# A hybrid block in split fp32 on one core: row factor one weight unit sooner, plain units made elsewhere

## The chip, the cores and the metric

The kernel runs on one core of one Trainium2 chip. The metric is device microseconds of one execution, as a median over runs. The chip's engines work from queues of their own: TensorE (PE in the profile, with its weight loads as PEld), VectorE (DVE), ScalarE (ACT), GpSimd (POOL), and SyncE (SP), which here issues the weight loads as DMAs.

## The reference

The input is 256 rows of 2048 values, in fp32, as are all weights. One layer is computed, and a last norm:

```python
x = x + 0.5 * swiglu_ffn(rms_norm(x, ffn1_norm), w_gate, w_up, w_down)   # d_ff = 5632
z = rms_norm(x, mix_norm) @ w_in                                         # 2048 x 5120
y = concat(rms_norm(lru part of z), rms_norm(short-convolution part of z))
x = x + y @ w_out
x = x + 0.5 * swiglu_ffn(rms_norm(x, ffn2_norm), ...)
return rms_norm(x, final_norm)

rms_norm(x, gain) = x * rsqrt(mean(x * x) + 1e-6) * gain
swiglu_ffn(x)     = (silu(x @ w_gate) * (x @ w_up)) @ w_down
```

The recurrent part of the mixer needs softplus(-lambda) of a parameter vector of 1024 values.

## The kernel before, in words

**Split fp32.** A product of two fp32 matrices is made from three matmuls of rounded parts: each operand is hi + lo, where ScalarE casts hi and VectorE subtracts to get lo. Weights come in units of four 128-row blocks by 512 columns (1 MB, tile `raw`); `parts_of` makes `hi` (two casts of 128x1024) and `lo` (one subtraction of 128x2048, in FFN1's opening two of 128x1024), and `multiply` issues the matmuls: for each of the two row tiles 4 x 2 with hi and 4 with lo. A unit for both row tiles is 24 matmuls of 128x512. The rows of x (2048 columns = 16 blocks = 4 units) lie transposed in `xT[u]`, each unit as hi and lo side by side.

**The norm.** `Norm.turn` transposes x on PE into PSUM (`pt`); ScalarE writes hi from there, times the gain, VectorE lo. `Norm.squares` sums the squares on ScalarE (`junk`). `Norm.factor` makes the row factor r, one value for each row of x, by a square root on ScalarE (`s`) and small steps on VectorE. `Norm.rows` spreads r over the partitions: two steps on VectorE make diagonals (`diag`), matmuls with ones make `pb`, and VectorE copies it to `bc`.

**An FFN.** The first 512 columns of gate and up are made from xT that is not yet normalised (u = 0..3, each first with gate, then with up: g0, u0, g1, ... in the text); r is applied to the result. The other ten blocks of 512 columns go by pairs, five times `seven` for gate and for up, every second time followed by `down`. `seven` computes 2 row tiles x 2 column blocks over two units of x by seven products instead of eight, as in Strassen's scheme (p0 to p6 in the names), and the other two units as usual (x0, x1 in the names, with the column block behind). For the products it needs the first two units normalised and four sums of them; `seven_of` makes the sums and their hi and lo parts (`xs`). `normalise(u)` makes a unit normalised: per row tile it adds hi and lo into an fp32 tile `v`, multiplies by bc, casts hi and subtracts lo (`x`). On the weights' side, `seven` subtracts raw units from one another on VectorE (`raw <- raw, raw`). Each seven has four PSUM banks a, c, e, d.

**Order.** A tile scheduler reorders instructions within each engine by its own estimates; `Engine.pinned` keeps the written order, in FFN1's opening up to unit 1's up block. Small work for later is put into a queue by `defer` with a cost, and `pump` takes from it after each weight unit; `flush` empties it. In FFN1's opening x itself is being loaded, and transposes and squares of unit u+1 go between weight units; in FFN2's they have been deferred from the mixer's end. `turns` are the transposes of the parameter vectors, called in FFN1 after the second pair, and `prepare` computes the softplus and halves two biases, deferred to the mixer. The buffers: raw units 3 (and 2 kept in an FFN), hi and lo 2 each (and 1 more in an FFN), PSUM 8 banks.

All instructions carry line 42 in the profile, that of the wrapper that records them; they are told apart by tile names, in which the profile leaves out numbers.

Of the kernel before, what the change touches and what calls it, by code (L numbers as in the profile page):

```python
# [48 lines left out]
def hybrid_block(ctx: ExitStack, tc: tile.TileContext, a: dict, out: bass.AP):  # L49
# [157 lines left out]
    class Norm:  # L207
# [12 lines left out]
        def turn(self, ks):  # L220
            for k in ks:
# [8 lines left out]
                act.activation(hi, pt, AF.Copy, scale=g)  # L230
                dve.scalar_tensor_tensor(lo, pt, g, f32(hi), op0=ALU.mult, op1=ALU.subtract)
# [76 lines left out]
    def seven_of(x0, x1, v, spare, parts):  # L308


        a11, a12, a21, a22 = v[0, 0], v[0, 1], v[1, 0], v[1, 1]
        dve.tensor_tensor(spare, a21, a22, op=ALU.add)
        dve.tensor_tensor(a21, a11, a21, op=ALU.subtract)
        dve.tensor_tensor(a11, spare, a11, op=ALU.subtract)
        dve.tensor_tensor(a12, a12, a11, op=ALU.subtract)
        sf = {0: stationary(x0, 0), 1: stationary(x1, 0), 3: stationary(x1, 1)}
        for (i, q), (hi, lo) in zip(((4, spare), (5, a11), (6, a21), (2, a12)), parts):
            act.copy(hi, q)
            dve.tensor_tensor(lo, q, f32(hi), op=ALU.subtract)
            sf[i] = [(hi[:, j, :], lo[:, j, :]) for j in range(UK)]  # L320
        return sf
# [4 lines left out]
    def seven(w, rows, cols, sf, xs, name, keep, done, between=None):  # L326
# [32 lines left out]
        s5 = snap(c, "s5")  # L359
        usual(0, b2, 1, (e, 1, True, not two), (c, 0, False, False))  # L360
        if between:
            between()
        dve.tensor_tensor(w11, w22, w11, op=ALU.subtract)
        product_of(5, w11, a)
        u2 = snap(a, "u2")
        if two:
# [16 lines left out]
    def ffn(tag, norm, after, opening=False):  # L383
        with tc.tile_pool(name=f"ffn{tag}", bufs=1) as fp:
# [32 lines left out]
            xs, vs, sf = [], {}, {}  # L417

            def normalise(u):

                xs.append(big(f"x{tag}_{u}"))
                for t in range(NT):
                    hi, lo = (slice(o + t * P, o + (t + 1) * P) for o in (0, S))
                    v = vs[t, u] = quad(keep(f"v{tag}_{u}_{t}"))
                    x = f32(norm.xT[u])
                    dve.tensor_tensor(v, x[:, :, hi], x[:, :, lo], op=ALU.add)
                    dve.tensor_tensor(v, v, norm.bc[:, hi].unsqueeze(1).to_broadcast([P, UK, P]), op=ALU.mult)
                    act.copy(xs[u][:, :, hi], v)
                    dve.tensor_tensor(xs[u][:, :, lo], v, f32(xs[u][:, :, hi]), op=ALU.subtract)
                if u == 1:  # L430
                    pair = [big(f"xs{tag}_{i}") for i in range(2)]
                    sf.update(
                        seven_of(
                            xs[0], xs[1],
                            vs,
                            quad(keep(f"spare{tag}")),
                            [(b[:, :, o : o + P], b[:, :, o + P : o + S]) for b in pair for o in (0, S)],
                        )
                    )

            ps = {(m, t): bank(f"ps_{m}{tag}_0_{t}") for m in "gu" for t in range(NT)}
            Engine.pinned = opening
            for u in range(KD // UK):
                for m, w in (("g", wg), ("u", wu)):
# [17 lines left out]
                    if opening and u < 3 and m == "u":  # L462
                        norm.turn(range(4 * u + 4, 4 * u + 8))
                        if u == 0:
                            norm.squares(0)
                        norm.squares(u + 1)
                        if u == 2:
                            norm.factor()
                    multiply([(ps[m, t], stationary(norm.xT[u], t), u == 0, u == 3) for t in range(NT)], blk)
                    pump(1.5)  # L470
                    if (u, m) == (1, "u"):
                        Engine.pinned = False
                        flush()
                        if not opening:
                            norm.factor()
                    elif (u, m) == (2, "u" if opening else "g"):
                        norm.rows()
                        normalise(0)
                    if u == 3:
                        for k in range(len(xs), len(xs) + 2):  # L480
                            if k < 4:
# [421 lines left out]
```

## Time and profile before

| | |
|---|---|
| median of 3 runs | 1771.69 us (1770.08 to 1773.82) |
| the profiled execution | 1770.94 us, its span 1769.0 us |
| mean granted clock of TensorE | 0.995 |
| PE, DVE, ACT busy | 98%, 85%, 59% of the span |
| moved by DMA | 343 MB, mean 194 GB/s |

Times in the timelines are in us from the start of the span. An entry in brackets is the time for which the engine sat idle ahead of the instruction, and the engine and tile that released it. FFN1 lies from 0 to 724 us, the mixer to 1049, and FFN2 behind it.

### The profile page before, as it was taken

What the parts mean: (1) busy time and instruction counts of PE and PEld (TensorE: products, weight loads), DVE (VectorE), ACT (ScalarE), POOL (GpSimd) and SP (SyncE); (2) the same over time, 40 slices, a digit from 0 to 9 for tenths busy, and PEclk for the clock granted to TensorE, in tenths of its full rate; (3) what the DMA queues carried; (4) which work ended last, traced back from release to release, by engine and by line L of the source; (5) the groups of instructions that cost most, each with busy time, mean ns of one, the idle gap of its engine ahead of it and who ended that gap; (6) DMA issues with size and microseconds to landing.
All of it is one profiled execution on the core that took longest, in us unless ns stands there. A gap on an engine that the chain in (4) does not pass through costs nothing. (4 is left out here: it accounts for less than half of the span.)

```text
span 1769.0 us, 20338 instructions
## 1 busy us (share of the span) xinstructions
PE 1739.7 (98%) x8031; PEld 1436.8 (81%) x8031; DVE 1495.7 (85%) x1252; ACT 1047.6 (59%) x1350; POOL 7.0 (0%) x32
## 2 busy tenths in 40 slices
PE   8999999999999999999999998999999999999998
PEld 7778788888888888888888886888788888888886
DVE  6998989988789888688987667989799887899895
ACT  6665566665466656565665454666466564566654
POOL 1000000000000000000000000000000000000000
PEclk9999999999999999999999999999999999999999
DMA  9274565575556556456555663574566547555752
GB/s 334 82 247 164 204 208 190 191 261 186 171 192 212 194 187 210 160 170 199 167 191 188 240 206 103 191 239 161 194 223 205 203 145 248 190 191 190 241 185 98
DMA packets 173904, 343.24 MB, mean 194 GB/s; under 512 B 5620, under 2 KB 8048, under 8 KB 173680
## 3 DMA queue, kind: packets, MB, share of 16 engines
q1 hardware_dynamic: 173344, 340.82, 56.9%
q8 instruction: 63, 1.03, 0.2%
q10 hardware_dynamic: 144, 1.05, 0.1%
q14 instruction: 33, 0.27, 0.0%
q0 software_dynamic: 320, 0.07, 0.0%
HBM read 339.82 MB, written 2.10 MB: 193 GB/s over the span
## 5 line engine op out<-in xcount | busy, mean ns | idle before, releaser
L42 PE MATMUL ps_in<-xT_nm,hi_in 128*128 128x512 f32 x640 | 225.0, 397 | 0.2 <-ACT hi_in L42 0.2
L42 ACT CAST hi_g_p<-raw_g 128x1024 fp32r<-128x1024 f32 x140 | 142.5, 1049 | 113.6 <-DVE raw_g L42 50.1
L42 DVE TENSOR_TENSOR lo_g_p<-raw_g,hi_g_p 128x2048 fp32r<-128x2048 f32 x70 | 160.0, 2288 | 34.8 <-ACT hi_g_p L42 34.0
L42 ACT CAST hi_u_p<-raw_u 128x1024 fp32r<-128x1024 f32 x140 | 141.2, 1049 | 72.7 <-PE ps_u_a L42 28.2
L42 PE MATMUL ps_in<-xT_nm,lo_in 128*128 128x256 f32 x640 | 178.6, 281 | 1.6 <-DVE lo_in L42 1.6
L42 DVE TENSOR_TENSOR lo_u_p<-raw_u,hi_u_p 128x2048 fp32r<-128x2048 f32 x70 | 159.2, 2287 | 19.3 <-ACT hi_u_p L42 19.1
L42 PE MATMUL ps_d<-hi_d,h 128*128 128x512 f32 x704 | 169.6, 392 | 0.0
L42 PEld LDWEIGHTS ps_d<-hi_d,h 128*128 128x128 f32 x704 | 131.5, 188 | 28.2
L42 PEld LDWEIGHTS ps_in<-xT_nm,hi_in 128*128 128x128 f32 x640 | 119.9, 188 | 28.6 <-ACT hi_in L42 0.6
L42 ACT CAST hi_d<-raw_d 128x1024 fp32r<-128x1024 f32 x88 | 88.2, 1048 | 69.2 <-PE ps_u_d L42 22.7
L42 DVE TENSOR_TENSOR lo_d<-raw_d,hi_d 128x2048 fp32r<-128x2048 f32 x44 | 100.6, 2290 | 33.1 <-ACT hi_d L42 33.1
L42 PEld LDWEIGHTS ps_in<-xT_nm,lo_in 128*128 128x128 f32 x640 | 120.4, 189 | 2.8 <-DVE lo_in L42 2.7
L42 ACT CAST hi_in<-raw_in 128x1024 fp32r<-128x1024 f32 x80 | 81.6, 1049 | 63.6 <-PE ps_in L42 44.7
L42 DVE TENSOR_TENSOR lo_in<-raw_in,hi_in 128x2048 fp32r<-128x2048 f32 x40 | 91.3, 2284 | 31.3 <-ACT hi_in L42 31.2
L42 ACT CAST hi_d_p<-raw_d 128x1024 fp32r<-128x1024 f32 x84 | 84.4, 1047 | 55.8 <-DVE raw_d L42 34.3
L42 DVE TENSOR_TENSOR lo_d_p<-raw_d,hi_d_p 128x2048 fp32r<-128x2048 f32 x42 | 95.5, 2289 | 17.8 <-ACT hi_d_p L42 17.7
L42 ACT CAST hi_g_x<-raw_g 128x1024 fp32r<-128x1024 f32 x80 | 81.1, 1049 | 39.4 <-PE ps_g_c L42 24.0
L42 ACT CAST hi_u_x<-raw_u 128x1024 fp32r<-128x1024 f32 x80 | 80.7, 1049 | 36.0 <-PE ps_u_c L42 25.1
L42 DVE TENSOR_TENSOR raw_g<-raw_g,raw_g 128x2048 f32<-128x2048 f32 x40 | 91.4, 2288 | 8.3 <-DMA raw_g<-in_ffn_w_gate_dram 7.8
L42 DVE TENSOR_TENSOR raw_u<-raw_u,raw_u 128x2048 f32<-128x2048 f32 x40 | 91.6, 2290 | 7.9 <-DMA raw_u<-in_ffn_w_up_dram 7.3
L42 DVE TENSOR_TENSOR lo_g_x<-raw_g,hi_g_x 128x2048 fp32r<-128x2048 f32 x40 | 91.4, 2286 | 2.2 <-ACT hi_g_x L42 1.9
L42 DVE TENSOR_TENSOR lo_u_x<-raw_u,hi_u_x 128x2048 fp32r<-128x2048 f32 x40 | 91.5, 2286 | 1.0 <-ACT hi_u_x L42 0.4
(348 smaller groups left out, 3604.3 us busy)
## 6 DMA issues: line engine op xcount, KB each, us to landing
raw_u<-in_ffn_w_up_dram SPq DMA_DIRECT2D x88, 1024.0 KB, 5.2
raw_d<-in_ffn_w_down_dram SPq DMA_DIRECT2D x88, 1024.0 KB, 5.1
raw_g<-in_ffn_w_gate_dram SPq DMA_DIRECT2D x87, 1024.0 KB, 5.2
raw_in<-in_w_in_dram SPq DMA_DIRECT2D x40, 1024.0 KB, 5.1
raw_o<-in_w_out_dram SPq DMA_DIRECT2D x16, 1024.0 KB, 5.1
xres<-in_x_dram SPq DMA_DIRECT2D x4, 512.0 KB, 8.1
fin<-in_final_norm_dram ACTq DMA_DIRECT2D x1, 1024.0 KB, 5.5
out_dram<-xres SPq DMA_DIRECT2D x4, 256.0 KB, 2.7
```

Of the source, the lines that this page charges most:

```text
L42: ins = getattr(self.engine, name)(*args, **kwargs)
```

## The change

- `Norm.turn` can let ScalarE write the fp32 tiles `v` from the transposed x in PSUM as well, one row tile at a time. FFN1's opening asks for it for units 2 and 3.
- In FFN1's opening, the squares, the factor and the transposes of unit 3 come ahead of unit 2's gate block instead of its up block, and the rows behind the gate block instead of the up block.
- In FFN2, the deferred work is flushed behind unit 0's gate block, the factor is made behind unit 0's up block and the rows behind unit 1's gate block (before: flush and factor behind unit 1's up block, rows behind unit 2's gate block).
- `normalise` no longer adds hi and lo; `plain(u)` does so, at a place of its own. A table `follow` says what comes behind which block.
- `seven_of` makes the sum for product 4 first, and returns a function for the rest, which the first gate `seven` calls behind product 4; unit 3 is normalised behind product 5.
- `turns` and `prepare` move to FFN1's second `down`; the polynomial in `prepare` is written with fused steps (8 fewer).

```diff
@@ -217,7 +217,8 @@
                     junk, xres[:, t, c * CW : (c + 1) * CW], AF.Square, accum_out=self.ss[:, t, c : c + 1]
                 )
-        def turn(self, ks):
+        def turn(self, ks, plain=None):
             for k in ks:
                 pt = bank(f"pt_{self.name}_{k}")[:, :S]
                 for t in range(NT):
@@ -228,6 +229,9 @@
                 xT = self.xT[k // UK][:, k % UK, :]
                 hi, lo = xT[:, :S], xT[:, S:]
                 act.activation(hi, pt, AF.Copy, scale=g)
+                if plain:
+                    for t in range(NT):
+                        act.activation(plain[t][:, k % UK, :], pt[:, t * P : (t + 1) * P], AF.Copy, scale=g)
                 dve.scalar_tensor_tensor(lo, pt, g, f32(hi), op0=ALU.mult, op1=ALU.subtract)
         def later(self, c):
@@ -305,20 +309,32 @@
-    def seven_of(x0, x1, v, spare, parts):
+    def seven_of(sf, x0, x1, v, spare, parts):
         a11, a12, a21, a22 = v[0, 0], v[0, 1], v[1, 0], v[1, 1]
-        dve.tensor_tensor(spare, a21, a22, op=ALU.add)
-        dve.tensor_tensor(a21, a11, a21, op=ALU.subtract)
-        dve.tensor_tensor(a11, spare, a11, op=ALU.subtract)
-        dve.tensor_tensor(a12, a12, a11, op=ALU.subtract)
-        sf = {0: stationary(x0, 0), 1: stationary(x1, 0), 3: stationary(x1, 1)}
-        for (i, q), (hi, lo) in zip(((4, spare), (5, a11), (6, a21), (2, a12)), parts):
+        parts = iter(parts)
+        def split(i, q):
+            hi, lo = next(parts)
             act.copy(hi, q)
             dve.tensor_tensor(lo, q, f32(hi), op=ALU.subtract)
             sf[i] = [(hi[:, j, :], lo[:, j, :]) for j in range(UK)]
-        return sf
+        sf.update({0: stationary(x0, 0), 1: stationary(x1, 0), 3: stationary(x1, 1)})
+        dve.tensor_tensor(spare, a21, a22, op=ALU.add)
+        split(4, spare)
+        def rest():
+            dve.tensor_tensor(a21, a11, a21, op=ALU.subtract)
+            dve.tensor_tensor(a11, spare, a11, op=ALU.subtract)
+            split(5, a11)
+            split(6, a21)
+            dve.tensor_tensor(a12, a12, a11, op=ALU.subtract)
+            split(2, a12)
+        return rest
     def quad(tile):
         return tile.rearrange("p (j c) -> p j c", j=UK)
@@ -357,12 +373,16 @@
         dve.tensor_tensor(w11, w12, w11, op=ALU.subtract)
         product_of(4, w11, c, True)
         s5 = snap(c, "s5")
+        if between:
+            between(0)
         usual(0, b2, 1, (e, 1, True, not two), (c, 0, False, False))
         if between:
-            between()
+            between(1)
         dve.tensor_tensor(w11, w22, w11, op=ALU.subtract)
         product_of(5, w11, a)
         u2 = snap(a, "u2")
+        if between:
+            between(2)
         if two:
             usual(1, b3, 1, (e, 1, False, True), (c, 0, False, False))
         dve.tensor_tensor(w12, w22, w12, op=ALU.subtract)
@@ -414,30 +434,59 @@
                     turn_hidden(*waiting.pop(0))
-            xs, vs, sf = [], {}, {}
+            units, vs, sf = [], {}, {}
+            def room(u):
+                for t in range(NT):
+                    vs[t, u] = quad(keep(f"v{tag}_{u}_{t}"))
+                return {t: vs[t, u] for t in range(NT)}
+            def plain(u):
+                x = f32(norm.xT[u])
+                for t, v in room(u).items():
+                    dve.tensor_tensor(
+                        v, x[:, :, t * P : (t + 1) * P], x[:, :, S + t * P : S + (t + 1) * P], op=ALU.add
+                    )
             def normalise(u):
-                xs.append(big(f"x{tag}_{u}"))
+                if u == len(units):
+                    units.append(big(f"x{tag}_{u}"))
                 for t in range(NT):
                     hi, lo = (slice(o + t * P, o + (t + 1) * P) for o in (0, S))
-                    v = vs[t, u] = quad(keep(f"v{tag}_{u}_{t}"))
-                    x = f32(norm.xT[u])
-                    dve.tensor_tensor(v, x[:, :, hi], x[:, :, lo], op=ALU.add)
+                    v = vs[t, u]
                     dve.tensor_tensor(v, v, norm.bc[:, hi].unsqueeze(1).to_broadcast([P, UK, P]), op=ALU.mult)
-                    act.copy(xs[u][:, :, hi], v)
-                    dve.tensor_tensor(xs[u][:, :, lo], v, f32(xs[u][:, :, hi]), op=ALU.subtract)
-                if u == 1:
+                    act.copy(units[u][:, :, hi], v)
+                    dve.tensor_tensor(units[u][:, :, lo], v, f32(units[u][:, :, hi]), op=ALU.subtract)
+            def sums():
+                if not left:
                     pair = [big(f"xs{tag}_{i}") for i in range(2)]
-                    sf.update(
-                        seven_of(
-                            xs[0], xs[1],
-                            vs,
-                            quad(keep(f"spare{tag}")),
-                            [(b[:, :, o : o + P], b[:, :, o + P : o + S]) for b in pair for o in (0, S)],
-                        )
-                    )
+                    halves = [(b[:, :, o : o + P], b[:, :, o + P : o + S]) for b in pair for o in (0, S)]
+                    left.append(seven_of(sf, units[0], units[1], vs, quad(keep(f"spare{tag}")), halves))
+                else:
+                    left.pop()()
+            left = []
+            if opening:
+                follow = {
+                    (0, "u"): [lambda: plain(0)],
+                    (1, "u"): [flush, lambda: plain(1)],
+                    (2, "g"): [norm.rows, lambda: normalise(0)],
+                    (2, "u"): [lambda: normalise(1), sums],
+                    (3, "g"): [lambda: normalise(2)],
+                }
+            else:
+                follow = {
+                    (0, "g"): [flush],
+                    (0, "u"): [norm.factor, lambda: plain(0)],
+                    (1, "g"): [norm.rows, lambda: plain(1), lambda: normalise(0)],
+                    (1, "u"): [lambda: normalise(1), sums, lambda: plain(2)],
+                    (2, "g"): [lambda: normalise(2), lambda: plain(3)],
+                }
             ps = {(m, t): bank(f"ps_{m}{tag}_0_{t}") for m in "gu" for t in range(NT)}
             Engine.pinned = opening
             for u in range(KD // UK):
@@ -459,30 +508,21 @@
                     if opening and u < 2 and m == "u":
                         load_x(u + 2)
                     blk = parts_of(raw, n, ((0, 2), (2, 4)), (lambda i: None) if opening else None)
-                    if opening and u < 3 and m == "u":
-                        norm.turn(range(4 * u + 4, 4 * u + 8))
-                        if u == 0:
-                            norm.squares(0)
-                        norm.squares(u + 1)
+                    if opening and u < 3 and m == ("u" if u < 2 else "g"):
                         if u == 2:
+                            norm.squares(3)
                             norm.factor()
+                        norm.turn(range(4 * u + 4, 4 * u + 8), room(u + 1) if u else None)
+                        for c in ((0, 1), (2,), ())[u]:
+                            norm.squares(c)
                     multiply([(ps[m, t], stationary(norm.xT[u], t), u == 0, u == 3) for t in range(NT)], blk)
                     pump(1.5)
                     if (u, m) == (1, "u"):
                         Engine.pinned = False
-                        flush()
-                        if not opening:
-                            norm.factor()
-                    elif (u, m) == (2, "u" if opening else "g"):
-                        norm.rows()
-                        normalise(0)
-                    if u == 3:
-                        for k in range(len(xs), len(xs) + 2):
-                            if k < 4:
-                                normalise(k)
-            for k in range(len(xs), 4):
-                normalise(k)
-            xs = list(enumerate(xs))[2:]
+                    for fn in follow.get((u, m), ()):
+                        fn()
+            units.append(big(f"x{tag}_3"))
+            xs = list(enumerate(units))[2:]
             for t in range(NT):
                 sg = keep(f"sg{tag}_0_{t}")
                 act.activation(sg, ps["g", t], AF.Silu, scale=norm.r[:, t : t + 1])
...
@@ -524,6 +566,8 @@
                                 for i in range(NT):
                                     update(2 - b, i, *got[i, b])
+                        if tag == 1 and m == 5:
+                            prepare()
                         seven(wd, (m, n), (2 * CW, CW), sh, [(u, hidden[u]) for u in us[:-2]], f"d{tag}_{m}", keep, add)
                 hidden.clear()
                 turned.clear()
@@ -551,13 +595,16 @@
                         settle()
                     waiting.append((1 + 2 * s + n, t, sg[t, n], s % 2 == 0))
-                seven(wg, (0, 1), cs, sf, xs, f"g{tag}_{s}", keep, gate, settle)
+                def meanwhile(i):
+                    if i == 1:
+                        settle()
+                    elif s == 0:
+                        (sums, lambda: normalise(3))[i // 2]()
+                seven(wg, (0, 1), cs, sf, xs, f"g{tag}_{s}", keep, gate, meanwhile)
                 seven(wu, (0, 1), cs, sf, xs, f"u{tag}_{s}", keep, up)
                 if s % 2 == 0:
                     down(s == 4)
-                elif s == 1 and tag == 1:
-                    for t in turns:
-                        t()
             extra.clear()
@@ -567,6 +614,8 @@
     sp2, hba, hbi = small("sp2"), small("hba"), small("hbi")
     def prepare():
+        for t in turns:
+            t()
         lam = vec["lru_lambda"]
         m, e, den, sr, s2, pl = (small(f"lam_{n}") for n in ("abs", "exp", "den", "s", "s2", "poly"))
@@ -576,14 +625,12 @@
         dve.reciprocal(den, den)
         dve.tensor_tensor(sr, e, den, op=ALU.mult)
         dve.tensor_tensor(s2, sr, sr, op=ALU.mult)
-        dve.tensor_scalar(pl, s2, 2.0 / 17, 2.0 / 15, op0=ALU.mult, op1=ALU.add)
-        for d in (13, 11, 9, 7, 5, 3, 1):
-            dve.tensor_tensor(pl, pl, s2, op=ALU.mult)
-            dve.tensor_scalar(pl, pl, 2.0 / d, None, op0=ALU.add)
-        dve.tensor_tensor(pl, pl, sr, op=ALU.mult)
-        dve.tensor_scalar(sp2, lam, -1.0, 0.0, op0=ALU.mult, op1=ALU.max)
-        dve.tensor_tensor(sp2, sp2, pl, op=ALU.add)
-        dve.tensor_scalar(sp2, sp2, 2.0, None, op0=ALU.mult)
+        dve.tensor_scalar(pl, s2, 2.0 / 17, None, op0=ALU.mult)
+        for d in (15, 13, 11, 9, 7, 5, 3):
+            dve.scalar_tensor_tensor(pl, pl, 2.0 / d, s2, op0=ALU.add, op1=ALU.mult)
+        dve.scalar_tensor_tensor(pl, pl, 2.0, sr, op0=ALU.add, op1=ALU.mult)
+        dve.tensor_scalar(sp2, lam, -2.0, 0.0, op0=ALU.mult, op1=ALU.max)
+        dve.scalar_tensor_tensor(sp2, pl, 2.0, sp2, op0=ALU.mult, op1=ALU.add)
         dve.tensor_scalar(hba, vec["lru_b_a"], 0.5, None, op0=ALU.mult)
         dve.tensor_scalar(hbi, vec["lru_b_i"], 0.5, None, op0=ALU.mult)
...
-        defer(5.0, prepare)
```

More of the change, by code (lines that the diff above doesn't have):

```diff
@@ L513, in down @@
                     if c == 0:
-                        sh = seven_of(
-                            hidden[m], hidden[n], {(t, i): turned[u, t] for t in range(NT) for i, u in ((0, m), (1, n))},
+                        sh = {}
+                        seven_of(
+                            sh, hidden[m], hidden[n],
+                            {(t, i): turned[u, t] for t in range(NT) for i, u in ((0, m), (1, n))},
                             quad(keep(f"hspare{tag}_{m}")),
                             [[quad(keep(f"hs{tag}_{m}_{i}_{z}", F32R)) for z in range(2)] for i in range(4)],
-                        )
+                        )()
                         got = {}
```

## The prediction

> **What bounds the kernel now.** I read the page's busy table first, then the waits of TensorE (PE), the table by windows around the two longest ones, and the timelines of PE and VectorE (DVE) there.
>
> ```profile
> PE 1739.7 (98%) x8031; PEld 1436.8 (81%) x8031; DVE 1495.7 (85%) x1252; ACT 1047.6 (59%) x1350; POOL 7.0 (0%) x32
> ```
>
> PE is the bound: of the 1769.0 us span it idles 29.3. Nothing in the change removes matmuls worth naming, so only that idle time, and time at a lowered clock, can be won. The waits of PE (total, times, longest):
>
> ```profile
> PE ps_g_a L42 <- DVE lo_g_p L42: 4.7, 1, 4.7
> PE ps_g_e L42 <- ACT x L42: 3.4, 1, 3.4
> ...
> PE ps_g_c L42 <- ACT hi_g_p L42: 1.6, 1, 1.6
> PE ps_in L42 <- DVE lo_in L42: 1.6, 3, 0.9
> PE ps_g_a L42 <- ACT u_g L42: 0.9, 1, 0.9
> PE ps_d_a L42 <- DVE lo_d_p L42: 0.7, 1, 0.7
> PE ps_g_e L42 <- DVE x L42: 0.7, 1, 0.7
> ```
>
> About 6 us of start and 8.8 us of end stay. The rest lies mostly where each FFN goes from its first column block (raw units, row factor applied to the result) to the seven-product scheme (normalised units). In the PE timeline these places are (start, duration, then the idle time ahead in brackets):
>
> ```profile
> 65.82 0.49 PE L42 MATMUL ps_g_e<-hi_g_x,x 128*128 128x512 f32 x1 [3.35 <-ACT x L42]
> 66.97 3.36 PE L42 MATMUL ps_g_e<-hi_g_x,x 128*128 128x512 f32 x7 [0.66 <-DVE x L42]
> ```
> ```profile
> 1101.40 2.07 PE L42 MATMUL ps_g_a<-lo_g_p,x 128*128 128x512 f32 x4 [4.73 <-DVE lo_g_p L42]
> 1105.10 3.42 PE L42 MATMUL ps_g_c<-hi_g_p,xs 128*128 128x512 f32 x8 [1.62 <-ACT hi_g_p L42]
> ```
>
> Four matmuls take 1.08 elsewhere, not 2.07; eight take 2.01, not 3.42; seven some 1.75, not 3.36. So behind these gaps the clock fell, and the table by windows shows it (columns: span, PE, PEld, DVE, ACT and POOL busy, granted clock, DMA):
>
> ```profile
> 60.00:70.00 10.00, 5.99 (x19) 4.25 (x18) 9.97 (x18) 8.48 (x13) 0.00 (x0) 0.84 0.00 0
> 1100.00:1110.00 10.00, 6.98 (x20) 5.08 (x21) 9.91 (x5) 5.82 (x7) 0.00 (x0) 0.66 0.00 0
> ```
>
> At stake: FFN1 0.17+3.35+0.66 and 0.94 at 92 us, 5.1 idle, plus 1.6 of clock: 6.7. FFN2 4.73+1.62 plus (2.07-1.08)+(3.42-2.01): 8.8. Together 15.5 us, 0.9%. In both windows DVE is full (9.97, 9.91), so it is DVE's queue that is late. Its timeline shows why in FFN2:
>
> ```profile
> 1067.27 2.29 DVE L42 TENSOR_TENSOR lo_u<-raw_u,hi_u 128x2048 fp32r<-128x2048 f32 x1 [3.19 <-ACT hi_u L42]
> 1072.78 2.29 DVE L42 TENSOR_TENSOR lo_g<-raw_g,hi_g 128x2048 fp32r<-128x2048 f32 x1 [3.22 <-ACT hi_g L42]
> 1078.22 2.29 DVE L42 TENSOR_TENSOR lo_u<-raw_u,hi_u 128x2048 fp32r<-128x2048 f32 x1 [3.15 <-ACT hi_u L42]
> 1080.43 0.42 DVE L42 COPY bc_n<-pb_n 128x256 f32<-128x256 f32 x1
> ```
>
> DVE sat idle 1.03+3.19+3.22+3.15 = 10.6 us before the broadcast (bc), and nothing that needs bc could start.
>
> **The change, part by part.** The sum is made against the profiled execution, 1770.94 us (span 1769.0 and 1.94 around it), which is 0.75 below the median of the runs, 1771.69.
>
> *FFN2's opening.* The factor was already there (r at 1060.07, the diagonals by 1060.8), but the broadcast's matmuls stood behind a weight block at 1077.80. Now they stand two blocks of 5.5 us earlier, at 1066.9, and bc is copied behind the next lo_u, at 1069.9 instead of 1080.43. DVE then has 18 small steps at a pitch of 0.60 (10.8 us), that is to 1080.7; lo of g3 and u3 and of product 0 at 2.20 each end at 1082.9, 1085.1, 1087.3. PE wants the last at 1096.5 and got it at 1101.4: 9 us of lead instead of 4.7 us of lag. Following the new order: raw difference 1090.1; lo of product 4 by 1095.3 (wanted 1099.3); lo of the usual unit x01 by 1100.1 (1103.9); product 5 by 1106.7 (1108.3); normalised unit 3, now made between these, by 1109.1 (1109.2); product 6 by 1115.7 (1116.5). The last two leads are a few tenths, so a late cast costs some. By this the column's product 2 ends at 1120.2 instead of 1129.4. Gain 9, of 6 to 9.2: the low end puts 1.5 us of wait at each of the two tight places.
>
> *FFN1's opening.* Here the row factor waits for x itself. Before, s_n ended at 37.87, the diagonals at 39.45, but their matmuls stood behind a block, at 44.93 (bc 47.54). Now the squares, factor and transposes of unit 3 go ahead of the g2 block, and the broadcast behind it, at 39.55. For that the chain on ScalarE (ACT) must not lengthen, yet it gets 16 copies of 128x128 from PSUM (the plain units 2 and 3), and 10 of them stand ahead of s_n. No row has this shape: a step of 128x2 has a pitch of 0.11, one of 128x256 0.365. The latter is the nearer shape, at twice the elements, so I take 0.26: 2.6 us, covered by 1.24 us that ACT idled at 29.4 for a load and by the two casts of g3 (1.9 us), which now stand behind s_n. Then the diagonals are ready at 39.45 and pb waits for nothing. At 0.365 they come at 40.6 and PE waits 1.1; at 0.11 nothing changes. I keep 0 to 1.3.
>
> bc then comes at 42.75, behind unit 3's four subtractions (0.41 each) and half a lo of g3 (1.15). DVE saves the four additions of units 2 and 3 (4 x 0.60 = 2.4 us; units 0 and 1 were added early before, too), and fills an idle 2.04 us at 43.3. But it stays full to about 121 us, where the before-trace first shows it idle (0.71). Following its queue: lo of u3 by 54.0 (wanted 54.5), product 0 by 56.2 (58.15), then PE waits 0.95 near 59 for product 4's cast, 1.05 near 62 for the usual unit's, and 2.5 near 70 for unit 3, whose normalisation now stands behind a raw difference of 2.20. Those 4.5 us stand against the 6.7 from above, 2.2 won; followed step by step to the end of this first column, past small waits that go too, PE is 3.5 us ahead. Then the next column's raw tiles are only loaded as their buffers come free (issue near 94, 5.2 to landing, differences near 101), and lo of its product 5 holds PE at 118.0 where it was 119.85: 1.9 kept. Between 1.9 and 3.5 I take 2.5, as some of that order will move. Range 0 to 4.5 (0 if the copies cost the 1.3 as well).
>
> The 2.5 us gap decides about the clock. Gaps of 0.66 and 0.94 left it at 1.00, those of 3.35 and 4.73 did not; no row lies between. I take no drop; with one it is 1.6 less.
> [...]
>
> *The parameter steps* (two transposes with copies, some 28 tiny steps of 0.2 pitch, 8 of them gone) move from the up columns and the mixer's queue to FFN1's down stage near 405 to 425 us. Both places have PE without a gap; DVE's lead there on product 5 is 1.4 us (ready 416.9, wanted 418.3), and its queue waits 2.6 for casts. 20 steps of 0.2 are 4 us of queue, the lead and those 2.6 cover them. Cost 0, to 2 without that cover.
>
> *The mixer.* With that entry gone from its queue of deferred work, gates come about one weight unit earlier, ahead of some lo_in. PE's waits there sum to 1.8 us. An early gate step delays a lo_in that PE wants next (a reciprocal of 128x256 is 1.75), a removed one frees it. I take 0, of -1.8 to +3.
>
> Sum: 1770.94 - 9 - 2.5 = 1759.4; plus the 0.75 to the median of runs 1760.2, told as 1760.
>
> **Rivals.**
> - *Both openings without any wait and at full clock*: 15.5 less, 1756.2, and 1754 with the mixer's waits gone. Against it: DVE is full in FFN1 to 121 us and sheds only 2.4.
> - *FFN1 trades one wait for another, FFN2 gains*: unit 3's late normalisation and the casts cost all that the earlier bc brings, the clock falls: 1771.7 - 9 = 1763, or 1766 with FFN2 at its low end. For it: 4.5 us of new waits by my own queue.
> - *FFN2's lead is given back*: the raws' three buffers hold loads back, so PE runs into DMA later in the column; 1771.7 - 2.5 - 3 = 1766. The 1120 to 1130 window moved 250 GB/s at a DMA share of 0.78, so there is room.
> [...]
> - *It does nothing*: the scheduler keeps the old places. The new instruction order has the pb matmuls in the new ones, so I give this almost nothing.
>
> **How the numbers follow.** Forecast 0.55 (1757.5 to 1764), no waits at all 0.12, FFN1 trades 0.15, lead given back 0.08, slower 0.06, near no change 0.04. Runs of this kernel spread 0.2% (1770.08 to 1773.82), 3.5 us: that bounds "no change", 1768.2 to 1775.2. Faster holds the first four cases less some of their tail: 0.87; same 0.06; slower 0.07. The range for 8 in 10 goes from 1755, a little under the case without waits, to 1766.5, which takes in the trades and the FFN2 low end with the opening's 1.3.
>
> **What would show it.** In the changed profile: pb's matmuls near 39.6 and 1066.9, bc near 43 and 1070; no idle PE and clock 1.00 between 1080 and 1120; DVE's idle gaps at 1067 to 1078 filled; a PE gap of 2 to 3 us near 70 with releaser x; s_n ending by 38. ACT rows of 128x128 at 0.2 to 0.3. Wrong would be: pb waiting for diag over 2 us, a clock under 0.9 near 70 or 1105, lo_d_p waits near 418, or lo_in waits above 4 us.

## The result and the profile after

The changed kernel takes 1757.7 us, the median of 4 runs (1755.88 to 1759.12), where the kernel before takes 1772.76: ratio 0.9915, 95% interval 0.9897 to 0.9933, so some 0.85% less and clear of the spread. In a later measurement the ratio was 0.9914 (0.9900 to 0.9927). The first profiled execution took 1759.12 us, its span 1757.3; the second profile has 1755.4.

The busy table of the page, and PE's waits (total, times, longest):

```profile
PE 1735.2 (99%) x8031; PEld 1434.5 (82%) x8031; DVE 1491.3 (85%) x1240; ACT 1050.3 (60%) x1366; POOL 6.9 (0%) x32
```
```profile
PE ps_g_c L42 <- DVE x L42: 2.3, 1, 2.3
PE ps_in L42 <- DVE lo_in L42: 1.6, 2, 1.2
PE ps_g_e L42 <- ACT hi_g_x L42: 0.8, 1, 0.8
PE ps_d_a L42 <- DVE lo_d_p L42: 0.8, 2, 0.6
PE ps_g_c L42 <- ACT hi_g_p L42: 0.7, 1, 0.7
```

The waits of 4.7, 3.4 and 1.6 at the two openings are gone. What has come instead is FFN1's: 0.7 at 60 us, 0.8 at 63 and 2.3 at 73. In the windows that lost most, PE is now full in FFN2, at full clock, and still waits in FFN1 (columns as in the prediction: the granted clock is the third number from the end):

```profile
60.00:70.00 10.00, 8.85 (x41) 6.92 (x42) 9.93 (x12) 8.97 (x14) 0.00 (x0) 1.00 0.02 3
70.00:80.00 10.00, 7.62 (x32) 5.58 (x32) 10.00 (x8) 4.32 (x6) 0.00 (x0) 1.00 0.52 179
1090.00:1100.00 10.00, 10.00 (x46) 8.19 (x45) 10.00 (x8) 6.72 (x9) 0.00 (x0) 1.00 0.27 77
1100.00:1110.00 10.00, 10.00 (x49) 8.33 (x48) 9.93 (x9) 7.43 (x11) 0.00 (x0) 1.00 0.40 135
```

VectorE's timeline in FFN2 shows why. Only one of the long idle gaps is left (3.19); behind the copy to bc stand the small steps where the next gaps were:

```profile
1057.69 2.29 DVE L42 TENSOR_TENSOR lo_g<-raw_g,hi_g 128x2048 fp32r<-128x2048 f32 x1 [1.07 <-ACT hi_g L42]
1063.18 2.29 DVE L42 TENSOR_TENSOR lo_u<-raw_u,hi_u 128x2048 fp32r<-128x2048 f32 x1 [3.19 <-PE pb_n L42]
1065.39 0.42 DVE L42 COPY bc_n<-pb_n 128x256 f32<-128x256 f32 x1
1065.84 1.90 DVE L42 TENSOR_TENSOR v<-v,bc_n 128x512 f32<-128x512 f32 x3
```

**A ledger by stages.** PE does the same matmuls in all kernels, so the time at which it begins a stage, taken from the PE timelines, says how far one execution is ahead of the first profile of the kernel before. The table has the gain of each stretch in us, that is by how much the lead grew in it (minus: it shrank):

| | first profile after | second profile after | second profile before |
|---|---|---|---|
| start to 16 us | -0.2 | 0.0 | -0.3 |
| FFN1's opening and first gate pair, to 107 us | +3.0 | +1.8 | -0.6 |
| first up pair, to 149 us | -0.7 | -0.1 | 0.0 |
| rest of FFN1, to 724 us | +0.3 | +0.4 | 0.0 |
| mixer and out-projection, to 1050 us | +1.7 | +2.5 | +1.0 |
| FFN2's opening and first gate pair, to 1146 us | +9.1 | +9.1 | -0.8 |
| rest of FFN2, to 1738 us | -1.5 | -0.1 | -0.1 |

By the mean of the two profiles each, 13.1 us were won (spans 1769.45 and 1756.35); the runs say 15. Two profiles of a kind do not place a sum better than that: in the experiments' runs the spans of the kernel before spread from 1768.0 to 1772.2, and those of the changed one in its runs from 1754.1 to 1757.3. The 1.5 lost behind FFN2's opening, too, are of one execution only, waits of 0.57 us at 1245 and 0.19 at 1699 among them; the second profile loses 0.1 there.

### The profile page after: what moved, and what is told of

Same layout as the page of the kernel before. It is cut to its first block, busy times and chain, and to the rows that moved or that the text cites. A ratio compares the mean times of both kernels' runs of the same rounds, so it can differ in the third digit from the quotient of the medians.

```text
span 1757.3 us, 20323 instructions
## 1 busy us (share of the span) xinstructions
PE 1735.2 (99%) x8031; PEld 1434.5 (82%) x8031; DVE 1491.3 (85%) x1240; ACT 1050.3 (60%) x1366; POOL 6.9 (0%) x32
## 3 DMA queue, kind: packets, MB, share of 16 engines
q10 hardware_dynamic: 144, 1.05, 0.1%
## 5 line engine op out<-in xcount | busy, mean ns | idle before, releaser
L42 ACT CAST hi_in<-raw_in 128x1024 fp32r<-128x1024 f32 x80 | 81.6, 1050 | 62.5 <-PE ps_in L42 48.4
```

The lines of the kernel that those rows point to most:

```text
L42: ins = getattr(self.engine, name)(*args, **kwargs)
```

## The experiments

All were made from the changed kernel. "Ahead" is meant as in the ledger, "the pair" or "first gate pair" of FFN1 is its stretch from 16 to 107 us, and "the stretch" in FFN2 that from 1050 to 1146; ratios are to the kernel before. Where an interval overlaps the 0.9900 to 0.9927 of the changed kernel, as in experiments 1, 3, 4, 7, 11 and 12, or only just misses it, as in 6 and 8, the runs alone hardly tell the two kernels apart, and the reading rests on the profile.

**1. FFN1's opening back.**

```diff
-                    if opening and u < 3 and m == ("u" if u < 2 else "g"):
+                    if opening and u < 3 and m == "u":
...
-                    (2, "g"): [norm.rows, lambda: normalise(0)],
...
+                    (2, "u"): [norm.rows, lambda: plain(0), lambda: normalise(0)],
+                    (3, "g"): [lambda: plain(1), lambda: normalise(1), sums, sums, lambda: plain(2), lambda: normalise(2)],
+                    (3, "u"): [lambda: plain(3), lambda: normalise(3)],
```

> FFN1's opening goes back to its old places (unit 3's transposes, squares and factor ahead of u2, rows behind u2, additions on VectorE, all sums and unit 3 ahead of the seven products); FFN2, the parameter steps and the mixer stay as changed. Theory (each opening pays by itself, FFN1 about 2.9 us by the two profiles: from -0.44 at 56 us to 2.4 at 724 us): span 1757.3 + 2.9 = 1760.2 us, the waits of 3.35 and 0.66 near 66 us and the lowered clock (0.84 in 60 to 70 us) are back, FFN2's opening has no wait. Rival (what FFN1 wins is given back later, and only FFN2 counts): span within 1 us of 1757.3.

Ratio 0.9935 (0.9923 to 0.9948), median 1760.03, span 1760.0. The waits near 66 us are back (2.78 and 0.57), and FFN1's first gate pair loses 2.1 us against the first profile of before. In the windows of 4 us the clock was 0.73, 0.50 and 0.50 from 64 to 76 us. The loss is larger than that of either profile of before, as the clock stayed down longer: 10.2 us here, an estimate from these windows and the 0.99 behind them, with 0.50 as its value while it is down; 3.4 and 6.8 there (experiment 10). The theory holds: the span is the 1760 that it gave, and FFN2 still gains its 9.1.

**2. FFN2's opening back.**

```diff
-                    (0, "g"): [flush],
-                    (0, "u"): [norm.factor, lambda: plain(0)],
...
+                    (1, "u"): [flush, norm.factor],
+                    (2, "g"): [norm.rows, lambda: plain(0), lambda: normalise(0)],
+                    (3, "g"): [lambda: plain(1), lambda: normalise(1), sums, sums, lambda: plain(2), lambda: normalise(2)],
+                    (3, "u"): [lambda: plain(3), lambda: normalise(3)],
```

> FFN2's opening goes back to its old places (flush and factor behind u1, rows behind g2, all sums and unit 3 ahead of the seven products); FFN1, the parameter steps and the mixer stay as changed. Theory (9.1 us come from this place): 9.1 us over the changed kernel, span 1766.4, with waits of 4.7 and 1.6 and the clock at about 0.66 in the ten us behind. Rival (1.4 us of it were given back in later columns of FFN2, so that these come back too): 7.7 us, span 1765.0, and no wait at 1245 to 1252 us beyond the 0.3 of before.

Ratio 0.9967 (0.9957 to 0.9977), median 1767.6 of 9 runs, span 1766.1. Waits of 2.21 and 4.65 us are back and the stretch loses 1.0 against before, so the new one is worth 9.1 to 10.1. This is the larger part of the change. The rival is out: its 1.4 us were the loss at the end of the changed kernel's first profile, which the second does not have. The clock fell behind the shorter wait already: it stands at 0.50 from 1096 us on, and the longer one began at 1095.6 (the wait in the first line, then the clock as the third number from the end):

```profile
1094.39 1.20 PE L42 MATMUL ps_g_a<-lo_g_p,x 128*128 128x512 f32 x4 [2.21 <-DVE lo_g_p L42]
```
```profile
1092.00:1096.00 4.00, 1.38 (x5) 0.67 (x4) 4.00 (x5) 1.75 (x4) 0.00 (x0) 0.98 0.00 0
1096.00:1100.00 4.00, 0.00 (x0) 0.00 (x0) 3.97 (x4) 1.07 (x2) 0.00 (x0) 0.50 0.00 0
```

**3. No plain units from ScalarE.**

```diff
-                        norm.turn(range(4 * u + 4, 4 * u + 8), room(u + 1) if u else None)
+                        norm.turn(range(4 * u + 4, 4 * u + 8))
...
-                    (3, "g"): [lambda: normalise(2)],
+                    (3, "g"): [lambda: plain(2), lambda: normalise(2), lambda: plain(3)],
```

> The plain fp32 units 2 and 3 of FFN1 are made by VectorE's additions again (4 x 0.60 us more on VectorE, 16 copies of 0.25 us less on ScalarE); all else as changed. Theory A (VectorE's queue bounds FFN1's first column pair): PE is about 2.4 us later at the end of the first gate column (104 us), of which 1 to 2.4 stay. Theory B (the loads of the up column's raw units, for which VectorE waited 2.7 us near 101, set the end): under 0.7 us stays. Theory C (the copies lengthen ScalarE's chain to the factor): the broadcast's matmuls come earlier by 0.2 us, as they waited for the diagonals before; worth 0.2.

Ratio 0.9932 (0.9920 to 0.9945), span 1757.9. The first gate pair gains 0.8 us instead of 1.8 to 3.0, and 0.8 is left at 149 us. That is theory A in its direction, 1.0 to 2.2 us. But part of it is a wait that none of the theories had, since the scheduler now sets half a lo of g3 and all of unit 3's subtractions among the small steps of the factor, ahead of the diagonals:

```profile
41.41 0.68 PE L42 MATMUL pb_n<-diag_n,ones 128*128 128x128 f32 x4 [1.72 <-DVE diag_n L42]
```

So C did not come true: with fewer steps on ScalarE the broadcast's matmuls came at 41.41, not 39.80. But s_n itself ended later (38.35, not 37.79), as unit 3's four steps were now set ahead of it. What the copies alone cost the chain is not shown by this run.

**4. Parameter steps at their old calls, and by that the old mixer order.**

```diff
-                        if tag == 1 and m == 5:
-                            prepare()
...
+                elif s == 1 and tag == 1:
+                    for t in turns:
+                        t()
...
+        defer(5.0, prepare)
```

> The parameter steps go back to their old calls (the transposes behind the second pair of FFN1, the polynomial deferred to the mixer, still in its shorter form); by that the mixer's instruction order is the old one on all three engines. Theory (the order of the mixer is worth 1.6 us, and the steps in the down stage cost 0.45): span 1757.3 + 1.6 - 0.45 = 1758.5, with a wait of 0.9 for lo_in near 870 us again. Rival (what the mixer won is chance of a run, such as its pace of 5.55 us a unit where it was 5.65): span 1756.9 to 1757.3, the pace between 797 and 842 us like that of the changed kernel.

In its profile (span 1756.5) the wait of 0.93 at 871 us is back, yet mixer and out-projection are 2.2 us ahead of the first profile of before, with the same order on all three engines (the second profile of before: 1.0). In the eleven profiles with the new order this stage is 1.2 to 3.7 ahead, though the kernels do not differ there. Two things make that spread. PE's waits for lo_in near 747 and 754 us sum to anything from 0 to 2.0 us in the eleven. And from 785 to 842 us the first profile of before took 57.57 us, where its second and this run, in the same order, took 56.65: 0.9 us of every lead in this stage is the slow stretch of the profile that it is measured against. So the 1.6 of one profile are within chance. But this profiled execution was the fastest of its five, and their ratio is 0.9936 (0.9923 to 0.9948) against 0.9914: some 4 us slower by the ratios, 2.3 by the medians, with intervals that just overlap. Whether the mixer's order is worth 0 or some us stays open.

The down stage is clear: in all nine profiles with the new place PE loses 0.45 us between 382 and 446 us, here 0.0. But between 255 and 340 us the same nine win 0.6, and here nothing is won. Of that, 0.36 us are the two transposes, which PE has to do at either place. Net 0.1.

**5. Early broadcast, but all sums and unit 3 ahead of the products, in both FFNs.**

```diff
-                    (3, "g"): [lambda: normalise(2)],
+                    (3, "g"): [lambda: normalise(2), sums],
+                    (3, "u"): [lambda: normalise(3)],
...
-                    (2, "g"): [lambda: normalise(2), lambda: plain(3)],
+                    (2, "g"): [lambda: normalise(2), lambda: plain(3)],
+                    (3, "g"): [sums],
+                    (3, "u"): [lambda: normalise(3)],
```

> In both FFNs the broadcast stays at its new place, but all four sums and unit 3 are made ahead of the seven products, as before, and not between them. Theory (the order of need matters where VectorE is full): in FFN1 some 8 us more stand ahead of lo of product 0, PE waits over 3.4 us near 59 us and the clock falls: 4 to 7 us lost; in FFN2, where the lead on product 4 is 4 us, 1.5 to 2 lost; span 1763 to 1766. Rival (only the broadcast's place matters): span within 1 us of 1757.3.

Ratio 0.9947 (0.9935 to 0.9960), span 1760.6. FFN1's first gate pair is 1.9 us behind the first profile of before; FFN2's still gains 8.1 of 9.1. The loss is less than the theory had (3.7 to 4.9 us in FFN1, where it gave 4 to 7, and 1.0 in FFN2, where it gave 1.5 to 2), and the span lies under its 1763 to 1766; the rival, no loss, is out. The wait was 5.43 us, and the clock was 0.64, 0.50 and 0.58 in the windows of 4 us from 60 to 72 us; that a fall takes a wait as long as the theory named is not shown, as it came behind 2.27 us in five profiles. The PE timeline in FFN1:

```profile
64.63 2.08 PE L42 MATMUL ps_g_a<-lo_g_p,x 128*128 128x512 f32 x4 [5.43 <-DVE lo_g_p L42]
68.32 3.51 PE L42 MATMUL ps_g_c<-hi_g_p,xs 128*128 128x512 f32 x8 [1.62 <-ACT hi_g_p L42]
```

So in FFN1 the early broadcast without the order of need wins nothing. In FFN2, where VectorE's lead is longer, the order is worth 1.0. The order of need without the early broadcast was not run.

**6. FFN2's broadcast one block later.**

```diff
-                    (1, "g"): [norm.rows, lambda: plain(1), lambda: normalise(0)],
-                    (1, "u"): [lambda: normalise(1), sums, lambda: plain(2)],
+                    (1, "g"): [lambda: plain(1)],
+                    (1, "u"): [norm.rows, lambda: normalise(0), lambda: normalise(1), sums, lambda: plain(2)],
```

> FFN2's broadcast goes one weight block later (behind u1, not g1); VectorE then does lo of g3 ahead of it, so its queue is 5.5 - 2.2, some 3.0 us behind the changed kernel's. Theory (the leads at unit 3 and product 6 are a few tenths, so the whole 3 us show): 2.5 to 3 us lost at about 1105 to 1112 us, in waits short enough that the clock stays at 1.00. Rival (the lead of 9 us on product 0 is what counts): no loss.

The stretch gains 6.2 instead of 9.1: 2.9 us lost, at one place in the PE timeline, and the clock stayed up (1.00 from 1092 to 1116 us):

```profile
1106.17 1.19 PE L42 MATMUL ps_g_a<-lo_g_p,xs 128*128 128x512 f32 x4 [2.26 <-DVE lo_g_p L42]
```

Ratio 0.9941 (0.9928 to 0.9953). The lead on product 0 is not what counts; the tight places behind it are. The wait fell on product 5, just ahead of the two places that the expectation named.

**7. Parameter steps behind FFN1's second pair.**

```diff
-                        if tag == 1 and m == 5:
-                            prepare()
...
+                elif s == 1 and tag == 1:
+                    prepare()
```

> The parameter steps go to FFN1's place behind the second pair (about 340 us), where their transposes were before; the mixer's order stays as changed. Theory (the steps cost 0.45 us in the down stage, where VectorE's lead is 1.4 us, and nothing where it idles for casts): 0.45 us less, span 1756.9; PE's lead on the kernel before stays at about 2.8 us from 382 to 724 us. Rival (that loss has another cause): the lead falls to 2.4 at 405 us as before, span 1757.3.

The loss in the down stage is gone (1.06 ahead at 382 us and at 468), so it did come from these steps. But the gain near 297 us is gone as well, and 0.5 more was lost between 214 and 255 us, where PE waited 0.27 at 220. Span 1757.1, ratio 0.9921 (0.9907 to 0.9935): no gain in all, as the ledger under 4 has it.

**8. The same, and unit 3's multiplications by GpSimd.**

```diff
-                    dve.tensor_tensor(v, v, norm.bc[:, hi]...
+                    (pool if opening and u == 3 else dve).tensor_tensor(v, v, norm.bc[:, hi]...
```

> As the one before, and in FFN1 GpSimd, which has nothing to do, makes the two multiplications of unit 3 by the broadcast (128x512 each). Theory (VectorE's queue of 42 to 100 us is the bound, and two of its steps of 0.60 go): the waits near 60 to 73 us (3.8 in all) shrink by about 1.2, of which 0.3 to 1.2 stay at 150 us. Rival (GpSimd slows VectorE while it works, or the loads near 101 us take it back): no gain, or VectorE's 128x512 steps of 0.69 take longer beside it.

The rival: ratio 0.9941 (0.9927 to 0.9954), median 1761.70 against 1758.38 of experiment 7, and the pair is 0.15 us behind the first profile of before. GpSimd takes 3.83 us for the two steps, and while it works three of VectorE's take 4.09 us, not the 1.89 that they take in the changed kernel. VectorE loses 2.2 us to be spared 1.2:

```profile
44.07 4.09 DVE L42 TENSOR_TENSOR v<-v,bc_n 128x512 f32<-128x512 f32 x3
```

**9. The changed kernel again.**

> The changed kernel once more, profiled again. In its first profile the wait of 2.28 us near 73 us left the clock at 1.00; in four later kernels with the same FFN1 (e2, e4, e6, e7) a wait of 2.27 there brought it to 0.67 to 0.91 for some us, and 1.2 us more were lost. Theory (it is chance whether the clock falls behind such a wait): FFN1's first gate column is 1.8 us (clock down) or 3.0 us (not) ahead of the kernel before, and nothing between; the mixer's lead over the first profile of the kernel before is 1 to 3.7 us with no cause in the kernel. Rival (these kernels differ by something else): as in the first profile, 3.0 and 1.6.

The wait is 2.27 and the clock goes to 0.82 and 0.75 in the two windows of 4 us from 72 to 80; the pair gains 1.8. The theory holds.

**10. The kernel before again.**

> The kernel before, profiled once more. The profiles account for 11.7 us of gain, the medians for 15. Theory (how long the clock stays down behind the waits at 66 and 1101 us is chance, and the first profile was a cheap case, as was its place among the runs): the same waits, but the clock down longer, and FFN1's opening, FFN2's opening or the mixer 1 to 3 us longer in all than in the first profile; span 1770 to 1772. Rival (the difference lies outside the span or in the runs of the changed kernel): span 1769.0 within 0.5, and the same three stages.

Between the two: FFN1's pair is 0.6 us longer and FFN2's stretch 0.8, with the same long waits and the clock down longer. In the first profile it stood at 0.50 from 66.9 to 70.3 us and from 1101.1 to 1107.9, 3.4 and 6.8 us. In the second the windows of 4 us have 0.65, 0.50 and 0.99 from 64 to 76 us, and 0.93, 0.50, 0.50 and 0.79 from 1096 to 1112: some 6.8 and 10.2 us, an estimate with 0.50 as its value while it is down. The mixer is 1.0 shorter. Span 1769.9. Eight matmuls behind the wait of 1.62 now took 3.78 us and the next four 1.58, where the first profile had 3.42 and 1.09:

```profile
1105.06 3.78 PE L42 MATMUL ps_g_c<-hi_g_p,xs 128*128 128x512 f32 x8 [1.62 <-ACT hi_g_p L42]
1108.64 1.58 PE L42 MATMUL ps_g_e<-hi_g_x,x 128*128 128x512 f32 x4
```

**11. Unit 3 ahead of the raw difference for product 5, in FFN1.**

```diff
                     if i == 1:
                         settle()
+                        if s == 0 and tag == 1:
+                            normalise(3)
-                    elif s == 0:
+                    elif s == 0 and (i, tag) != (2, 1):
```

> In FFN1 unit 3 is normalised ahead of the raw difference for product 5, not behind it; all else as changed. Theory (VectorE is full there, so the steps only change places, but PE has the unit's 16 hi matmuls to do meanwhile): the one wait of 2.28 us near 73 us becomes two shorter ones or goes, the clock stays at 1.00, and the first gate column is 1 to 2 us further ahead than the 1.8 of the kernels with the lowered clock; 0.5 to 1 of it is left at 150 us. Rival (the wait is VectorE's whole backlog): the same sum of waits, 3.8 us, in other places.

The 2.28 is 1.29 at 74 us, and 0.22 and 0.94 have come at 88 and 90 us: 3.9 in all, as the rival has it. But the clock stays at 1.00, and the pair gains 2.4, 0.6 more than with the lowered clock. Ratio 0.9914 (0.9900 to 0.9928), the same as the changed kernel's.

**12. FFN1's first gate pair by eight usual products.**

```diff
+    def eight(w, cols, us, name, done, between):
+        for n in (1, 0):
+            ps = [bank(f"ps_{name}_{t}{n}") for t in range(NT)]
+            for i, u in enumerate(us):
+                ...
+                multiply([(ps[t], stationary(u, t), i == 0, i == 3) for t in range(NT)], blk, True)
...
-                seven(wg, (0, 1), cs, sf, xs, f"g{tag}_{s}", keep, gate, meanwhile)
+                if tag == 1 and s == 0:
+                    eight(wg, cs, units, f"g{tag}_{s}", gate, ...)
```

> FFN1's first gate pair is made by eight usual products a column block and not by seven: PE gets 12 matmuls of 128x512 more (2.75 us), VectorE is freed of 4 raw differences and 3 lo (7 x 2.20 = 15.4 us) before 100 us, and the four sums are only wanted by the up pair. Theory (VectorE's queue bounds this pair, and the waits there are its backlog): no wait of PE between 57 and 105 us, clock 1.00, and no wait for the loads near 101 us, as the buffers come free earlier; against the changed kernel -3.8 - 1.2 + 2.75 = -2.2 us at 105 us, and up to 0.7 more by 150 us. Rival (the loads are the bound there, one megabyte for each 5.5 us block right behind the opening): waits for raw_g instead, and no gain or a loss of up to 2.75.

PE has no wait from 13 to 220 us, the clock is 1.00, and VectorE has room where it was full:

```profile
60.00:70.00 10.00, 10.00 (x50) 8.30 (x49) 9.93 (x9) 5.16 (x7) 0.00 (x0) 1.00 0.79 280
70.00:80.00 10.00, 10.00 (x46) 8.21 (x45) 6.98 (x7) 5.33 (x8) 0.00 (x0) 1.00 0.80 271
80.00:90.00 10.00, 10.00 (x46) 8.24 (x45) 4.59 (x2) 4.08 (x6) 0.00 (x0) 1.00 0.59 175
```

The pair gains 5.6 us, 2.6 to 3.8 more than the changed kernel, in spite of 2.75 us more of matmuls. Then 2.1 are given back in the second gate pair, where PE waits 1.2 us for a cast at 221. The median is 1756.51, ratio 0.9908 (0.9894 to 0.9921): the lowest of all, 0.75 us under the changed kernel run beside it, which is less than these runs can tell apart. VectorE's queue was the bound in this pair, and not the loads, for which PE never waited and VectorE 0.26 us, where it had waited 2.71 in the changed kernel.

## Why the prediction was right

The forecast was 1760 us, faster, in 1755 to 1766.5; 1757.7 was measured. Step by step:

- **FFN2's opening: right, by its own chain.** The step times were given in the time of the kernel before; the changed kernel stands 4.1 us earlier there. With that added, bc came at 1069.5 (told 1069.9), lo of product 0 was ready at 1087.5 (1087.3), of product 4 at 1095.5 (1095.3), of product 5 at 1106.8 (1106.7), unit 3 at 1109.4 (1109.1). PE did not wait, and gained 9.1 (9). Experiment 6 shows that the end of this chain is as tight as told, though its wait fell on product 5, for which the text had 1.6 us of lead, and not on the two places after it that it called tight.
- **FFN1's opening: right in kind, and in size without a fall of the clock.** s_n ended at 37.79 (told "by 38"), pb stood at 39.80 (39.55), bc at 42.55 (42.75). The waits came as 0.73, 0.75 and 2.28 (0.95, 1.05, 2.5), the last with the releaser x. The pair gained 3.0 (3.5), and 2.3 were left behind the up pair (1.9 to 3.5, taken 2.5), as VectorE waited there for a load as told. In the second profile, with the clock's fall, it was 1.8 and 1.7. The line is of the first profile:

```profile
103.44 2.29 DVE L42 TENSOR_TENSOR raw_u<-raw_u,raw_u 128x2048 f32<-128x2048 f32 x1 [2.71 <-DMA raw_u<-in_ffn_w_up_dram]
```

- **The copies on ScalarE: right.** A pair took 0.62 to 0.71 us, with a pitch of 0.25 each (told 0.26), and no wait of PE for the diagonals shows.
- **What I did not see: the place alone does not win FFN1, it takes the order.** The sum followed the queue in its new order, but the text gave the gain to the earlier bc and four saved additions. Experiment 5 has both, in the old order, and is 1.9 us behind; in experiment 3, with place and order but without the saved additions, 0.8 are still won in spite of a new wait of 1.72. What the order is worth without the place stays open.
- **The clock: right in the first profile, wrong as a rule.** "I take no drop; with one it is 1.6 less." Of six profiles with this pair (the changed kernel twice, experiments 2, 4, 6, 7) the clock fell in five, at a price of 1.2 us, not 1.6. One premise was misread: the gap of 0.66 did not leave the clock at 1.00, as it ended at 66.97 and the clock was at 0.50 from 66.9 to 70.3 us, behind the gap of 3.35. The fall shows in the eight matmuls behind the wait, in the PE timeline of experiment 2 and, as the last line and without it, of the changed kernel's first profile:

```profile
73.98 0.96 PE L42 MATMUL ps_g_c<-hi_g_x,x 128*128 128x512 f32 x3 [2.27 <-DVE x L42]
74.78 3.20 PE L42 MATMUL ps_g_a<-hi_g_p,xs 128*128 128x512 f32 x8
```
```profile
74.22 2.03 PE L42 MATMUL ps_g_a<-hi_g_p,xs 128*128 128x512 f32 x8
```

  That a gap of 2.5 us leaves the clock up was the author's estimate, from gaps of 0.94 and 3.35 in the trace of before; no run shows it. The runs had falls behind 2.27 us here and 2.21 in FFN2 in experiment 2, and none behind 2.28 in the first profile and 2.26 in experiment 6; from what length on a wait lowers the clock is not shown.
- **The parameter steps: right in sum, not in reason.** Cost 0 was told, since PE had no gap at either place. But 0.45 us were lost at the new place and 0.6 won at the old one, for the larger part by the two transposes (0.36), which are PE's own time: the term left them out. The lead on product 5 that it rests on, told as 1.4 us, is 2.2 in the trace of the kernel before (ready at 415.60, wanted at 417.82), which changes nothing in the conclusion.
- **The mixer: told as 0, of -1.8 to +3.** With the old order its profiles are 0 to 2.2 ahead (three), with the new one 1.2 to 3.7 (eleven), and the runs of experiment 4 lean to a gain of the new order without settling it.
- **Where the rest of the 15 us is: in part luck, in part open.** The sum was 11.5, made against one execution of the kernel before. By the means of the ledger the two openings won 2.3 (the first up pair taken in) and 9.5, where 2.5 and 9 were told; the mixer, told as 0, brought 1.6, and start and the rest of the FFNs cost 0.3. That is 13.1, and the 2 us between this and the runs are in no profile. The second profile of before shows both old openings dearer by 1.4 us in all, through the clock: the forecast did not count that a lowered clock has a spread in the kernel before as well.

Of the rivals, "FFN1 trades one wait for another" came nearest: 3.8 us of new waits came, 5.0 with the price of the clock's fall. But they stand against 6.7 of old waits and old clock, so that 1.8 to 3.0 were won. That FFN2's lead is given back did not show: of the 9.1, both profiles still have 9.0 at 1252 us.

## What to carry to other kernels

Where an engine idles before a broadcast and is full behind it, moving the broadcast's producer ahead of a block in PE's queue turns that idle time into lead, and it pays only up to the tightest later operand: follow the queue to the end of the full stretch, not to the first operand. Where the engine is full from the start, the place of the broadcast alone brings nothing; what counts is which operand comes first, and how much work there is at all, so that in one pair 2.75 us more of matmuls paid by sparing that engine 15, though over the whole kernel the runs cannot tell it from no gain. Make sums against more than one execution where a clock that falls in one execution and not in the next, here in five profiles of six, is part of what is to be won.

## What the runs showed of the hardware

- Behind a wait of 2.27 us on PE the granted clock fell in five of six profiles with the same instructions in this pair (price 1.2 us); in the sixth, with 2.28, it stayed at 1.00. It fell behind one of 2.21 in experiment 2 as well (0.98 in the window to 1096 us, 0.50 from there, with the next wait begun at 1095.6), while it stayed at 1.00 behind 2.26 in experiment 6 and 2.03 in experiment 8. Behind the six waits of 2.78 to 5.43 in the openings of both profiles of before and of experiments 1 and 5 it fell each time.
- How long the clock was down in the middle of the kernel: 3.4 us in FFN1 and 6.8 in FFN2 of the first profile of before, where it stood at 0.50 throughout. By the estimate from the windows of 4 us that experiments 1 and 10 have, it was 3.4 us behind each of the five waits of 2.27 (0.82 and 0.75 from 72 to 80 us in experiment 9, for one), 6.8 in FFN1 of the second profile of before, and 10.2 in that one's FFN2 and in experiments 1, 2 (FFN2) and 5.
- While GpSimd made two multiplications of 128x512 fp32 (3.83 us, experiment 8), three of VectorE's of the same shape took 4.09 us; in the changed kernel they took 1.89.
- PE's pace in the mixer differs by stretches: a weight unit of 32 matmuls took 5.55 or 5.65 us at a granted clock shown as 1.00 both times. From some 880 us to the end of the matmuls into ps_in near 955, all fourteen profiles have 5.65; from 797 to 842 us thirteen have 5.55, and only the first profile of the kernel before 5.65. What makes it so was not tried.
